# Lending input tiles to weight loads in the last mixer group of a two-layer backbone

## The chip, the cores and the metric

The kernel runs on one core of a Trainium2 chip. The metric is the device time of one execution in microseconds; three runs give a median. A profile of one further execution shows every instruction of the engines: TensorE (PE, its weight loads PEld), VectorE (DVE), ScalarE (ACT), GpSimd (POOL), and the queue of SyncE (SP or SPq), which issues nearly all transfers from HBM.

## The reference

Two layers of a trunk over 256 latent tokens and 256 context tokens of width 2048, with one batch. The first layer mixes by centred pooling, the second by neighbourhood attention; a gated MLP with a depthwise convolution of width 3 follows each (inner width 5504). Every sub-layer is preceded by an RMS norm and modulated by six vectors of 2048 per stream, which a product with `w_mod` gives. All is float32. What concerns the change is the first layer:

```python
def pool_mix(u, w, b, scale):          # windows 2, 4, 8, 16: four groups of 512 channels
    ...
    y = jnp.einsum('btgc,gcd->btgd', p, w).reshape(B, T, D) + b
    return y * scale

def conv_ffn(u, w_gate, w_up, conv_w, conv_b, w_down):
    gp = jnp.pad(u @ w_gate, ((0, 0), (1, 1), (0, 0)))
    gte = gp[:, :T] * conv_w[0] + gp[:, 1:T + 1] * conv_w[1] + gp[:, 2:] * conv_w[2] + conv_b
    return (jax.nn.silu(gte) * (u @ w_up)) @ w_down

ml = (silu_c @ w_mod[i] + b_mod[i]).reshape(B, 6, 1, D)
a_lat = modulate(rms_norm(h, norm1_g[i]), ml[:, 0], ml[:, 1])
h = h + ml[:, 2] * y_lat
h = h + ml[:, 5] * conv_ffn(modulate(rms_norm(h, norm2_g[i]), ml[:, 3], ml[:, 4]), ...)
```

The context stream `hc` goes through the same first layer with `silu_cc`.

## The kernel before, in words

Channels lie on the 128 partitions; the 16 tiles of 128 channels hold both streams side by side (512 columns). Each float32 operand of a large product is split in a high and a low part, and three matmuls (high by high, high by low, low by high) replace one. A weight load is a tile of 128 by 1024, 512 KB. `split` makes the high part by a cast on ScalarE (L143) and the low part by a subtraction on VectorE (L145).

The first layer is worked in four groups `g` of 512 channels, one for each pooling window. The modulation has 24 chunks of 512 outputs; a chunk is four quarters of two loads each (`wm`), multiplied on PE in strips of 32 columns (`mod`, L193), copied by ScalarE (`modev`, L198), and turned by four PE transposes (`modt`, L203). A row of the profile for `mod` counts two records for each matmul, so x8 is a whole quarter and x4 the half of one, that is, one load. `need(n)` has the modulation's generator run up to its n-th quarter. `mixer(g + 1)` prepares the next group's pooled input (tiles `ph`), multiplies by the pooling weights (`wp`, `pm`), adds to the streams, sums the squares for the second norm (`n2q`, `n2acc`), and leaves the group's four input tiles `Ad` in tiles A4g to A4g+3.

`partial(g, ...)` takes a group's input to the first eight tiles of the feed-forward's gate and up products, before the second norm is known. For the tiles 0 to 3 and then 4 to 7 it loads gate weights (`wcg`) and up weights (`wcu`), two loads of 512 KB each. Of the products, tiles 0 to 5 (`cg3_0` and so on) are added by VectorE into `part` (L558); tiles 6 and 7 (`cg_6`) stay in PSUM over all groups. Small products with the shift vectors (`pwg`, `pwu`, L528) use the unsplit loads and need `sh`, a copy of the shift chunk (12 to 15). A step is one tile of one of the two products; each is cut in two halves, and `between(half)` runs at the start of each half, 32 halves to a group: it asks for quarters of the modulation, takes a step of the mixer, and in the last group, from half 3, has the second norm finished (`n2s`, `n2b`, L299) and normalises the final inputs tile by tile (`normalise`, `nrm` L310, `A` L312 and L313) into the tiles A0 and up, one more every second half, so A4 from half 11 and A11 at half 25. GpSimd multiplies `part` by the norm (L352); gates follow at halves 16 to 25. The feed-forward's own loop (`gu0`, `g` and `u` L631 to L633) begins after the group; its two held tiles go through `late` (L355).

Loads take rooms in turn. There are six of their own (`wst`); `lend` adds tiles A that stand empty, and withdraws the others:

```python
    def lend(ks):
        rooms[:] = [r for r in rooms if r < 0 or r in ks] + [k for k in ks if k not in rooms]

    def stage(name):
        r = rooms.pop(0)
        rooms.append(r)
        if r >= 0:
            return ap0.tile([P, 1024], F32, tag=f"A{r}", name=name)
        return wst.tile([P, 1024], F32, tag=f"wst{-r}", name=name)
```

A load waits in the SP queue until the last reader of its room is done, and all loads behind it wait with it. Groups 0 to 2 have eight lent tiles beside the six (twelve ahead of group 0); at the last half of group 2 and in group 3 none is lent. The instructions are written in the order of these generators; the tile framework then sorts them by its own model of times, allots the rooms' waits, and each engine executes its list in that order.

Of the kernel before, what the change touches and what calls it, by code (L numbers as in the profile page):

```python
# [19 lines left out]
KT = D // P  # L20
# [16 lines left out]

NRH = 3
GATES = (16, 19, 22, 25)


_VEC = [
# [15 lines left out]
def kernel(ctx: ExitStack, tc: tile.TileContext, xT, cxT, wmod, wg, wu, wd, wp,  # L58
# [50 lines left out]
    def lend(ks):  # L109

        rooms[:] = [r for r in rooms if r < 0 or r in ks] + [k for k in ks if k not in rooms]
# [192 lines left out]
    def normalise(l, which, h_of, streams, rstd, pool, ks=range(KT), keep=A):  # L304

        for k in ks:
            a = ap0.tile([P, 2, 2, T], F32R, tag=f"A{k}", name=f"A{k}_{l}_{which}")
            y = pool.tile([P, 2, T], F32, tag="t2", name=f"nrm{l}{which}{k}")
            for s in streams:
                nc.vector.scalar_tensor_tensor(y[:, s], h_of(s)[:, k, :], M(l, which + 1, k, s),  # L310
                                               rstd[:, T * s : T * s + T], op0=ALU.mult, op1=ALU.mult)
                nc.scalar.activation(a[:, 0, s, :], y[:, s], AF.Identity, bias=M(l, which, k, s))  # L312
                ins = nc.vector.scalar_tensor_tensor(a[:, 1, s, :], y[:, s], M(l, which, k, s),  # L313
                                                     a[:, 0, s, :].bitcast(F32), op0=ALU.add, op1=ALU.subtract)
            keep[k] = a
            if l == 1 and k == 1:
                hold[:] = [ins.ins]
# [5 lines left out]
    with ExitStack() as ph0:  # L323
# [22 lines left out]
        def late(f):  # L346

            res = []
            for q in range(2):
                if f < NC:  # L350
                    r = PART[f][:, q]
                    nc.gpsimd.tensor_tensor(r, r, late_norm[0], op=ALU.mult)  # L352
                else:
                    r = f0.tile([P, 512], F32, tag="t2", name=f"late{f}_{q}")
                    nc.vector.tensor_tensor(r, HELD[f, q], late_norm[0], op=ALU.mult)  # L355
                for s in both:
                    v = r[:, T * s : T * s + T]
                    nc.scalar.activation(v, v, AF.Identity, bias=wsh[:, q, f, s : s + 1])
                res.append(r)
            return res  # L360

        def gate0(f, pg, pu):
            g1 = f0.tile([P, 2, T], F32, tag="t2", name=f"g1_{f}")
            nc.scalar.activation(flat(g1), pg, AF.Identity, scale=V("cw1_0")[:, f : f + 1], bias=V("cb_0")[:, f : f + 1])
            pg3 = pg.rearrange("p (s t) -> p s t", s=2)
            nc.vector.scalar_tensor_tensor(g1[:, :, 1:T], pg3[:, :, 0 : T - 1], V("cw0_0")[:, f : f + 1],
                                           g1[:, :, 1:T], op0=ALU.mult, op1=ALU.add)
            nc.vector.scalar_tensor_tensor(g1[:, :, 0 : T - 1], pg3[:, :, 1:T], V("cw2_0")[:, f : f + 1],
                                           g1[:, :, 0 : T - 1], op0=ALU.mult, op1=ALU.add)
            sg = f0.tile([P, 512], F32, tag="t2", name=f"sg_{f}")  # L370
            nc.scalar.activation(sg, flat(g1), AF.Silu)
            nc.vector.tensor_tensor(sg, sg, pu, op=ALU.mult)
            if f == NS - 1:
                a = mp.tile([P, 2, 512], F32R, tag="macc", bufs=1, name=f"act_{f}")
            else:
                a = act_tile(f"act_{f}", F32R)
            a = [a[:, 0], a[:, 1]]
            nc.scalar.copy(a[0], sg)
            nc.vector.tensor_tensor(a[1], sg, a[0].bitcast(F32), op=ALU.subtract)
            return a, sg  # L380
# [5 lines left out]
        with ExitStack() as phs:  # L386
# [45 lines left out]
            def need(n):  # L432
                while done[0] < n:
                    next(pump0, None)
                    done[0] += 1
# [4 lines left out]
            def mixer(g):  # L440
# [67 lines left out]
                yield  # L508

            def partial(g, sh, between):  # L510

                step = 0
                for fa in range(0, NS, 4):
                    for q, (nm, wsrc) in enumerate((("g", wg), ("u", wu))):
# [3 lines left out]
                        for j in range(4):  # L518
                            f = fa + j
                            between(2 * step)  # L520
                            if j == (3 if fa == 0 and q == 0 else 0):
                                need(20 * g + 21)
# [19 lines left out]
                            for i in range(4):  # L542
                                c = 512 * (j % 2) + P * i
                                xh, xl = flat(A[4 * g + i][:, 0]), flat(A[4 * g + i][:, 1])
                                nc.tensor.matmul(ps, hi[:, c : c + P], xh, start=(first and i == 0), stop=False)
                                nc.tensor.matmul(ps, hi[:, c : c + P], xl, start=False, stop=False)
                                nc.tensor.matmul(ps, lo[:, c : c + P], xh, start=False, stop=(final and i == 3))
                                if i == 1:
                                    between(2 * step + 1)
# [24 lines left out]
                next(mix)  # L574
            rstd = None
            for g in range(4):
                lend((range(8, KT), [*range(12, KT), *range(4)], range(8), ())[g])
                mix = mixer(g + 1) if g < 3 else None
                todo = [20 * g + 20 + n for n in STEPS] if g < 3 else []
                last = [14]  # L580
                F = {}
                rstd = n2.acc

                def between(half):
                    need(min(20 * g + LEAD + RATE * (half + 1) // 32, 20 * g + LEAD + PMAX))
                    if (g, half) == (2, 31):
                        lend(())
                    if g == 3 and half == NRH:
                        nc.scalar.copy(rstd, n2.rstd())
                        late_norm.append(rstd)  # L590
                    if todo and done[0] > todo[0] and half >= last[0] + 2:
                        last[0] = half
                        todo.pop(0)
                        next(mix)
                    k = (half - NRH) // 2
                    if g == 3 and 0 <= k < 12 and (half - NRH) % 2 == 0:
                        normalise(0, 3, h_of, both, rstd, f0, range(k, k + 1), keep=F)
                    if g == 3 and half in GATES:
                        e = GATES.index(half)
                        acts[e], _ = gate0(e, *late(e))  # L600

                partial(g, shs[g % 2], between)
                for n in todo:
                    need(n)
                    next(mix)
# [626 lines left out]
```

## Time and profile before

| what | value |
|---|---|
| time, median of three runs | 3102.35 us (3099.67 to 3103.05) |
| profiled execution, time | 3103.48 us |
| its span, first to last instruction | 3101.7 us |
| PE busy | 3030.0 us, 98% of the span |
| DVE, ACT, POOL busy | 1932.6, 1373.2, 826.1 us |
| moved from HBM | 554.93 MB, 180 GB/s over the span |

The span's start is zero for all times below. PE's busy share is near one nearly everywhere; where it idles, a view by stretches, the list of waits and the timelines of the engines tell. Group 3's first product begins near 352 us, and the feed-forward's loop at 454.54 us. Waits are put down to the instruction whose end came last. In a timeline, x counts merged records, and brackets give the idle time of the engine before a row and what ended it.

### The profile page before, as it was taken

Reading aid. Unit: us, or ns where it says so; the run is one execution under the profiler, and the core shown is the slowest. Engines: PE = TensorE matmul, PEld = TensorE weight load, DVE = VectorE, ACT = ScalarE, POOL = GpSimd, SP = SyncE. Lnnn points to the kernel's source line nnn. Section 1 sums busy time; section 2 is a strip of 40 time slices with the busy share of each in tenths; the row PEclk is TensorE's granted clock in tenths of the full one; section 3 lists DMA queues with packets and bytes.
Section 4 is the critical chain, followed back from the end, with each engine's and each line's share of the span. In section 5 each row is a group of like instructions: output and inputs, shape, how many; then the busy total and the mean of one; then the engine's idle time right before and its main releaser. Section 6 shows DMA issues by size and latency. Waiting matters only on the chain.

```text
span 3101.7 us, 40819 instructions
## 1 busy us (share of the span) xinstructions
PE 3030.0 (98%) x15082; PEld 2414.3 (78%) x15082; DVE 1932.6 (62%) x2748; ACT 1373.2 (44%) x2219; POOL 826.1 (27%) x823
## 2 busy tenths in 40 slices
PE   6999899999999999999999999999999999999998
PEld 2565558888888888888888788878788888888887
DVE  4445674285765848567485665564777666666666
ACT  3333454333233332323334444343545666656665
POOL 2011213213031230302213000000002466556665
PEclk9999999999999999999999999999999999999999
DMA  9978573264846657475573333332345565555563
GB/s 376 333 271 306 177 246 102 89 217 149 251 141 206 198 162 247 133 225 171 182 226 118 102 113 106 102 114 96 111 153 179 177 196 188 192 189 185 179 195 117
DMA packets 177927, 559.70 MB, mean 180 GB/s; under 512 B 17600, under 2 KB 22208, under 8 KB 177728
## 3 DMA queue, kind: packets, MB, share of 16 engines
q1 hardware_dynamic: 177728, 557.10, 55.0%
q8 instruction: 119, 1.95, 0.3%
q14 instruction: 80, 0.66, 0.1%
HBM read 554.93 MB, written 2.10 MB: 180 GB/s over the span
## 4 chain that ended last, share of the span: by engine, by line
PE 94%; DMA 2%; DVE 2%; POOL 1%; ACT 1%; issue 0%; SPq 0%; DVEq 0%; ACTq 0%; POOLq 0%
PE g L766 5%; PE u L766 5%; PE d L657 5%; PE d L659 5%; PE d L658 5%; PE d L813 4%; PE u L631 4%; PE u L632 4%; PE u L633 4%; PE g L631 4%; PE g L633 4%; PE g L632 4%; PE mod L193 3%; PE u L769 3%; PE g L769 3%; PE d L817 2%
## 5 line engine op out<-in xcount | busy, mean ns | idle before, releaser
L670 POOL TENSOR_TENSOR hl<-hl,dy 128x256 f32<-128x256 f32 x160 | 149.0, 931 | 958.6 <-ACT dy L669 957.3
L828 POOL TENSOR_TENSOR hl<-hl,dy 128x256 f32<-128x256 f32 x320 | 331.5, 1069 | 188.4 <-ACT dy L826 186.1
L241 DVE SCALAR_TENSOR_TENSOR macc<-wm,sc,macc 128x512 f32<-128x512 f32 (+1 forms) x360 | 325.2, 935 | 68.6 <-DMA wm<-wmod 67.6
L669 ACT ACTIVATE dy<-d,modT 128x256 f32<-128x256 f32 x320 | 133.5, 470 | 196.8 <-PE d L659 195.5
L193 PE MATMUL mod<-wm,sc 128*32 128x512 f32 x768 | 134.6, 618 | 26.6 <-DMA wm<-wmod 26.5
L670 POOL TENSOR_TENSOR hc<-hc,dy 128x256 f32<-128x256 f32 x160 | 126.0, 787 | 0.0
L145 DVE TENSOR_TENSOR wd_2l<-wd,wd_2h 128x1024 fp32r<-128x1024 f32 (+1 forms) x44 | 53.9, 1229 | 112.8 <-ACT wd_2h L143 112.8
L826 ACT ACTIVATE dy<-d,modT 128x512 f32<-128x512 f32 x160 | 104.4, 683 | 42.7 <-PE d L817 41.2
L915 POOL TENSOR_TENSOR rk<-rk,rp 128x256 f32<-128x256 f32 x16 | 13.2, 826 | 365.4 <-DVE rk L914 309.8
L145 DVE TENSOR_TENSOR wd_3l<-wd,wd_3h 128x1024 fp32r<-128x1024 f32 (+1 forms) x44 | 52.0, 1202 | 80.6 <-ACT wd_3h L143 80.6
L145 DVE TENSOR_TENSOR wd_1l<-wd,wd_1h 128x1024 fp32r<-128x1024 f32 (+1 forms) x44 | 53.7, 1224 | 58.6 <-ACT wd_1h L143 58.6
L466 POOL TENSOR_TENSOR pf<-ws,inv 128x256 f32<-128x256 f32 x32 | 27.7, 886 | 222.4 <-DVE ws L461 154.7
L193 PEld LDWEIGHTS mod<-wm,sc 128*32 128x32 f32 x768 | 23.6, 110 | 81.0 <-issue 59.4
L143 ACT CAST wd_1h<-wd 128x1024 fp32r<-128x1024 f32 (+1 forms) x44 | 45.2, 1029 | 79.8 <-PE u L632 50.6
L145 DVE TENSOR_TENSOR wd_0l<-wd,wd_0h 128x1024 fp32r<-128x1024 f32 (+1 forms) x44 | 54.6, 1247 | 40.7 <-ACT wd_0h L143 40.6
L1004 ACT ACTIVATE sb<-sb,nm 128x512 f32<-128x512 f32 x64 | 46.1, 721 | 64.4 <-DVE nm L1000 63.2
L143 ACT CAST wd_0h<-wd 128x1024 fp32r<-128x1024 f32 (+1 forms) x44 | 45.3, 1031 | 57.9 <-PE u L766 29.1
L792 DVE TENSOR_TENSOR actb<-sgb,actb 128x256 fp32r<-128x256 f32 x43 | 52.3, 1216 | 27.0 <-ACT actb L791 27.0
L657 PE MATMUL d<-act,wd_2h 128*128 128x512 f32 x172 | 68.0, 395 | 0.0
L658 PE MATMUL d<-act,wd_2h 128*128 128x512 f32 x172 | 67.9, 395 | 0.0
L657 PE MATMUL d<-act,wd_3h 128*128 128x512 f32 x172 | 67.9, 395 | 0.0
L657 PE MATMUL d<-act,wd_0h 128*128 128x512 f32 x172 | 67.9, 395 | 0.0
(1752 smaller groups left out, 9286.1 us busy)
## 6 DMA issues: line engine op xcount, KB each, us to landing
wm<-wmod SPq DMA_DIRECT2D x384, 512.0 KB, 6.1
wd<-wd SPq DMA_DIRECT2D x168, 512.0 KB, 4.4
wg<-wg SPq DMA_DIRECT2D x156, 512.0 KB, 4.6
wu<-wu SPq DMA_DIRECT2D x156, 512.0 KB, 4.5
wv<-wv SPq DMA_DIRECT2D x32, 512.0 KB, 3.9
wk<-wq SPq DMA_DIRECT2D x32, 512.0 KB, 4.0
wq<-wq SPq DMA_DIRECT2D x32, 512.0 KB, 3.7
wo<-wo SPq DMA_DIRECT2D x32, 512.0 KB, 4.4
```

Source lines behind the costliest of these rows:

```text
L145: eng.tensor_tensor(lo[:, :n], t[:, :n], hi[:, :n].bitcast(F32), op=ALU.subtract)
L193: nc.tensor.matmul(ps[32 * j : 32 * j + 32, :], sc[:, 4 * g + j, :], ts[j // 2][0][:, 512 * (j % 2) : 512 * (j % 2) + 512], start=(g == 0) ...
L241: nc.vector.scalar_tensor_tensor(acc[s], v, sc2[:, k, s : s + 1], acc[s], op0=ALU.mult, op1=ALU.add)
L631: nc.tensor.matmul(ps, hi[:, c : c + P], xh, start=(k == 0), stop=False)
L632: nc.tensor.matmul(ps, hi[:, c : c + P], xl, start=False, stop=False)
L633: nc.tensor.matmul(ps, lo[:, c : c + P], xh, start=False, stop=(k == KT - 1))
L657: nc.tensor.matmul(ps, hi[:, o : o + P], xh, start=(i == 0), stop=False)
L658: nc.tensor.matmul(ps, hi[:, o : o + P], xl, start=False, stop=False)
L670: nc.gpsimd.tensor_tensor(h_of(s)[:, k, :], h_of(s)[:, k, :], y[:, s], op=ALU.add)
L766: nc.tensor.matmul(ps, hi[:, c : c + P], flat(B[k]), start=(k == 0), stop=False)
L769: nc.tensor.matmul(ps[:, T:], lo[:, c : c + P], B[k][:, 0], start=False, stop=(k == KT - 1))
L828: nc.gpsimd.tensor_tensor(hl[:, k, :], hl[:, k, :], y[:, q], op=ALU.add)
```

## The change

At the last half of group 2 the eight tiles A4 to A11, the inputs of groups 1 and 2, are lent; from half 6 of group 3 only A8 to A11; from half 13 none. Before, nothing was lent from the last half of group 2 on. A4 is first written by the normalisation at half 11, A8 at half 19. No arithmetic is changed.

```diff
 NRH = 3
 GATES = (16, 19, 22, 25)
+
+LENT = {(2, 31): range(4, 12), (3, 6): range(8, 12), (3, 13): ()}
...
             for g in range(4):
-                lend((range(8, KT), [*range(12, KT), *range(4)], range(8), ())[g])
+                if g < 3:
+                    lend((range(8, KT), [*range(12, KT), *range(4)], range(8))[g])
                 mix = mixer(g + 1) if g < 3 else None
...
                 def between(half):
                     need(min(20 * g + LEAD + RATE * (half + 1) // 32, 20 * g + LEAD + PMAX))
-                    if (g, half) == (2, 31):
-                        lend(())
+                    if (g, half) in LENT:
+                        lend(LENT[g, half])
```

## The prediction

> **What bounds the kernel now.** The time before is 3102.35 us, the median of three runs from 3099.67 to 3103.05. The profiled execution took 3103.48 us, 1.13 more than the median, and 1.78 of it lie outside the span, which is the page's first line:
>
> ```profile
> span 3101.7 us, 40819 instructions
> ```
>
> I read the page first: TensorE (PE) is busy nearly everywhere, so a change to rooms for loads can only win where PE stands still. Next comes the view by stretches, over the stage that the change touches: from the first matmul of chunk 15 of the modulation to the first of the feed-forward's loop, 348 to 455 us. Columns: stretch, length, busy time of each engine, granted clock, share of the DMA engines, GB/s.
>
> ```profile
> core 0: us, PE busy (x) PEld busy (x) DVE busy (x) ACT busy (x) POOL busy (x), PEclk, DMA share, GB/s
> ...
> 362.00:376.00 14.00, 11.05 (x65) 6.62 (x67) 12.29 (x24) 4.25 (x9) 5.46 (x4) 1.00 0.31 111
> 376.00:392.00 16.00, 10.58 (x56) 5.90 (x50) 3.14 (x3) 5.69 (x11) 1.19 (x1) 0.79 0.77 261
> ...
> sum 107.00, PE 95.40 PEld 49.01 DVE 68.74 ACT 47.00 POOL 20.70; mean PE 15.90 PEld 8.17 DVE 11.46 ACT 7.83 POOL 3.45
> ```
>
> PE idles for 107.00 - 95.40 = 11.6 us, most of it from 362 to 392, where the DMA engines are first little used (0.31) and then crowded (0.77), and where the granted clock falls to 0.79. The list of waits of PE, from 360 to 456 us, accounts for all 11.6 (total, times, longest):
>
> ```profile
> PE pwu L528 <- DMA wcu<-wu: 5.4, 2, 4.1
> PE modt L203 <- ACT modev L198: 2.3, 2, 1.6
> PE pwg L528 <- ACT A L312: 1.6, 1, 1.6
> PE g L631 <- DVE late L355: 0.9, 1, 0.9
> PE mod L193 <- DMA wm<-wmod: 0.9, 2, 0.6
> PE n2b L299 <- DVE n2d L297: 0.5, 1, 0.5
> ```
>
> The queue's timeline (start, length of the issue, operation) tells why these weights are late:
>
> ```profile
> 349.90 0.33 SPq L127 DMA_DIRECT2D wm<-wmod  x1
> ...
> 369.83 0.33 SPq L127 DMA_DIRECT2D wm<-wmod  x1
> ...
> 376.20 0.38 SPq L127 DMA_DIRECT2D wcu<-wu  x1
> ```
>
> With six rooms, the load issued at 349.90 takes a room that PE has just left, the one at 369.83 the room of the group's gate weights, and `wcu` the room of that one: a chain of load, use, load in which PE is a link. `wcu` goes out at 376.20, and the pieces of PE that need it stand.
>
> **What the change does to it, by the built order of instructions.** Only the stretch from chunk 15 to the first two tiles of the feed-forward differs; every engine executes the same work. Eight loads take lent tiles: chunk 15's last two quarters in tiles 4 to 7, chunk 20's third in 8 and 9, the first `wcu` in 10 and 11. None lands in the four that stay lent longest: the rotation does not come round to them. So the effect is those eight loads, the six rooms left free by them, and a new order of what follows. PE's durations hold the rest of the prices:
>
> ```profile
> 340.40 0.39 PE L547 MATMUL cu<-Ad,wcu_4l 128*128 128x512 f32 x1
> ...
> 383.89 1.95 PE L528 MATMUL pwu<-wcu,sh 128*32 128x256 f32 x14 [4.13 <-DMA wcu<-wu]
> 385.77 0.80 PE L545 MATMUL cu<-Ad,wcu_0h 128*128 128x512 f32 x1
> ...
> 387.54 0.39 PE L547 MATMUL cu<-Ad,wcu_0l 128*128 128x512 f32 x1
> 387.76 0.40 PE L545 MATMUL cu<-Ad,wcu_0h 128*128 128x512 f32 x1
> ...
> 391.75 1.05 PE L193 MATMUL mod<-wm,sc 128*32 128x512 f32 x4
> 392.73 0.50 PE L546 MATMUL cu<-Ad,wcu_0h 128*128 128x512 f32 x1
> 393.07 0.40 PE L547 MATMUL cu<-Ad,wcu_0l 128*128 128x512 f32 x1
> ...
> 395.77 1.91 PE L193 MATMUL mod<-wm,sc 128*32 128x512 f32 x12
> ...
> 410.11 1.08 PE L528 MATMUL pwg<-wcg,sh 128*32 128x256 f32 x14
> ...
> 424.53 1.06 PE L193 MATMUL mod<-wm,sc 128*32 128x512 f32 x8
> ```
>
> The wait for `wcu`, 5.4 us. Tiles 10 and 11 come free with the last matmul of group 2 that reads them, the row at 340.40, which ends at 340.8. A load of `wcu` lands 5.5 us after its issue in the median here:
>
> ```profile
> wcu<-wu SPq DMA_DIRECT2D x4, 512.0 KB, 5.5
> ```
>
> So it is there at about 346.5. Before, PE came to it near 378 (383.89 less the two waits, 5.4, and the two matmuls between them), and it can come only a few microseconds sooner: over 25 us in hand. The wait goes: 5.4.
>
> The waits for `wm`, 0.9. Chunk 20's first and third quarters stand ahead of `wcu` in the queue, so they go out before 341; the second takes the rooms that are free at 349.90 and lands near 355.5. In the new order eight matmuls on each of two banks and the sums of the norm stand between chunk 15's end and the first of these, so PE needs none before about 359 (an estimate). Gone: 0.9.
>
> The clock. After the 4.1 us wait the 14 `pwu` took 1.95 us, where 14 of the same form take 1.08 (410.11): 0.87 lost. The four matmuls that follow took 387.54 - 385.77 = 1.77, where four take 4 x 0.22 (the step from 387.54 to 387.76) and 0.1 for the switch, 1.0: 0.77 lost. The longest wait left is 1.6 us, so I count 1.6 as won. The Trainium skill, "TensorE: Matmul & The Clock Gate", Part 1, says that the clock halves after about 3.4 us without work and returns after 3.4 us of it; its section on oscillation prices the throttled time at one half, which for two windows of 3.4 us would be an estimate of 3.4 us in place of my 1.6, and a gain 1.8 larger. I keep the rows, since part of the slow time fell on the wait itself.
>
> The wait for `n2d`, 0.5. Chunk 20's first three quarters now stand before the broadcast of the second norm on PE and cover DVE's chain. Gone; but the norm's result itself comes about 2 us later, since PE has 3 to 4 us of pieces in front. The wait before `pwg` (1.6) hangs on that norm's DVE work and on the copy of the shift: it stays, between 1 and 2; taken as unchanged.
>
> The waits for `modev`, 2.3. The first (0.7) was the copy of chunk 20 directly before its transposes; now eight matmuls, 1.8 us, stand between. The second (1.6) was ScalarE standing at the cast of the second `wcu` for its load, with the copy queued behind:
>
> ```profile
> 430.74 1.04 ACT L143 CAST wcu_4h<-wcu 128x1024 fp32r<-128x1024 f32 x1 [7.14 <-DMA wcu<-wu]
> ```
>
> In the new order the copy stands ahead of the cast, and six matmuls are between it and its transposes. Gone: 2.3.
>
> Pieces of the modulation. Half a quarter (x4, 1.05 us) costs as much as a whole (x8, 1.06), so cuts cost time. A piece set between other matmuls moves the second one after it to 393.07, where without it this would be 1.2 us earlier; a further quarter in the same piece adds 0.85 (1.91 for x12 less 1.06). Chunk 15's last quarter was two pieces and now joins the piece before: 2 x 1.2 - 0.85 = 1.55 won. Chunk 20's stays at two pieces, one of them newly between others: 0.2 lost. Chunks 20 (last) to 23 go from 21 pieces to 19 with the same units: 2 x 0.3 = 0.6 won. Sum 2.0 won; between 1 and 3.
>
> New waits. The load of chunk 15's last quarter now waits for DVE to be done with the pooling weights; chunk 15's second quarter is queued behind it on the queue. That split is done several microseconds before the queue moves on: nothing. The first half of `wcu`'s split now stands in the chain of the second norm (ScalarE 1.04 us for the cast): everything up to the tiles of group 3 comes 1.1 later there, covered by the 0.85 of the joined piece and a little slack: 0 to 0.3, taken as 0. The real one: the second `wcu`'s second half takes the room of a half of chunk 22 that now leaves PE in a later piece. From there to its use PE has about 5.6 us (two quarters 1.9, six matmuls 1.4, transposes 0.6 and 0.6, a quarter 1.1); landing takes 5.5 in the median: between 0 and 2, taken as 0.5, because the queue is quiet just then.
>
> What stays. The 0.9 before the feed-forward's first matmul: same order of DVE behind the last transposes.
>
> **The sum.** Waits 5.4 + 0.9 + 0.5 + 2.3 = 9.1; clock 1.6; pieces 2.0; less 0.5: 12.2 us. The profiled execution would be 3103.48 - 12.2 = 3091.3, the median 3102.35 - 12.2 = 3090.2. Bounds: with the low ends (clock 1.6, pieces 1, `wcu` 2, `pwg` 0.4 longer, 0.3 of the cast) 9.1 + 1.6 + 1 - 2.7 = 9.0; with the high ends 9.1 + 1.6 + 3 + 0.6 = 14.3.
>
> **The rivals.**
>
> The wait moves to the second `wcu`. The second half of the stage keeps six rooms and now runs on a PE that never pauses. Against: before, the same six rooms fed that half, and PE lost only the 1.6 us behind ScalarE's cast to them. For: the margin at the second `wcu` is near nothing, and PE comes to each room sooner. If PE waits there as long as it did for the second half of the first `wcu`, 4.1 us, and the clock's 1.6 is lost again, 12.7 - 5.7 = 7.0 us are won: 3095.3. Chance 0.17.
>
> VectorE becomes the bound. DVE is busy 68.74 us of 107.00; the stage would shrink to 95. Its normalisation stretches while GpSimd multiplies:
>
> ```profile
> 364.58 1.63 DVE L310 SCALAR_TENSOR_TENSOR nrm<-hl,modT,n2acc 128x256 f32<-128x256 f32 x1
> ...
> 367.64 0.47 DVE L310 SCALAR_TENSOR_TENSOR nrm<-hl,modT,n2acc 128x256 f32<-128x256 f32 x1
> ```
>
> 1.63 beside a product of GpSimd, 0.47 without. Twelve such products follow the norm; if each stretched two of DVE's instructions by 1.16 more than now, 28 us would be added, 2 more than DVE's 26 idle ones, and late starts in DVE's order would do the rest: some 8 us lost, 4 won, 3098.4, no difference that can be told. The Trainium skill, "GPSIMD Engine Reference", Specifications, says that GpSimd's SBUF interfaces are shared with VectorE and contended by instructions with two SBUF inputs; by it these two do collide, as the rows show. Against: most such meetings are in the 68.74 already. Chance 0.07.
>
> Slower: ScalarE stands in the second norm's chain. The cast of the first `wcu` is now before the last block of the sums of squares in ScalarE's order, at about 348.5. If its load were not there, ScalarE, then DVE, the norm and PE would wait one for one. It decides from a landing at 348.5, and it makes the kernel slower once the landing is past 348.5 + 12.2 = 360.7; at a landing of 370 it gives 3112. Against: issue near 339 to 341 by the row at 340.40, and few loads ahead. Chance 0.06.
>
> **How the numbers follow.** A measurement of this kernel can tell about 0.2%, 6.2 us. The forecast (9 to 14.3 won) has 0.70, the moved wait 0.17, both faster by more than that; VectorE 0.07, the same; ScalarE 0.06, slower. Faster 0.87, same 0.07, slower 0.06. Range: 14.3 won and 1.3 for the scatter of a median gives 3086.7; the other end reaches over the moved wait, to 3097.
>
> **What would show it.** Right: between 362 and 392 no wait of PE for `wcu` or `wm`; the clock 1.00 throughout; PE busy near 94 us of a stage near 95; `wcu` landed before 347; the first matmul of the feed-forward's loop about 12 us sooner in the span. A wait of PE for the second `wcu` above 1 us shows the first rival, waits of PE for DVE's `part` or `A` the second, ScalarE idle before its cast at 348 the third. The forecast is wrong if the stage shrinks by less than 9 us, or if it does and the later stages give it back.

## The result, and the profile after

The changed kernel took 3088.35 us, the median of six runs from 3086.2 to 3089.06, against 3101.76 us (3099.67 to 3104.05, six runs) for the kernel before, run on the same chip. The ratio is 0.9957, with a 95% interval of 0.9946 to 0.9968: 13.4 us won, where 12.2 were forecast. The profiled execution took 3089.06 us, 14.4 less than the one of before.

The page of the kernel after begins with the span, and its first part gives PE's busy time, which fell by 3.0 us while the span fell by 14.4: most of the gain is time in which PE had stood idle.

```profile
span 3087.3 us, 40828 instructions
...
PE 3027.0 (98%) x15082; PEld 2416.4 (78%) x15082; DVE 1932.3 (63%) x2748; ACT 1372.7 (44%) x2219; POOL 828.1 (27%) x823
```

The view by stretches, with the columns of the prediction's:

```profile
core 0: us, PE busy (x) PEld busy (x) DVE busy (x) ACT busy (x) POOL busy (x), PEclk, DMA share, GB/s
...
362.00:376.00 14.00, 12.43 (x88) 7.31 (x86) 11.70 (x21) 5.02 (x9) 4.18 (x3) 1.00 0.62 212
376.00:392.00 16.00, 16.00 (x87) 9.40 (x80) 10.63 (x20) 6.78 (x16) 5.49 (x4) 1.00 0.57 190
...
sum 93.00, PE 90.55 PEld 48.85 DVE 69.77 ACT 46.76 POOL 21.66; mean PE 15.09 PEld 8.14 DVE 11.63 ACT 7.79 POOL 3.61
```

From 376 to 392 PE is busy without a gap, where it had been busy for 10.58 of 16 us; the clock is 1.00 instead of 0.79; and the DMA engines, 0.31 and then 0.77 busy before, are evenly used (0.62, 0.57). The list of waits of PE is down to two lines, those that were forecast to stay:

```profile
engine line waited for: us in total, times, longest us
PE pwg L530 <- ACT A L314: 1.6, 1, 1.6
PE g L634 <- DVE late L357: 0.9, 1, 0.9
```

The timeline shows the shift products of the up weights without a wait in front, and the ends of the stage:

```profile
348.46 1.07 PE L195 MATMUL mod<-wm,sc 128*32 128x512 f32 x8
...
375.27 1.09 PE L530 MATMUL pwu<-wcu,sh 128*32 128x256 f32 x16
...
440.77 0.50 PE L634 MATMUL g<-A,wg_8h 128*128 128x512 f32 x1 [0.88 <-DVE late L357]
```

From here on "the stage" is the time from chunk 15's first matmul to the first of the feed-forward's loop. It was 454.54 - 347.95 = 106.6 us before and is 92.3 after: 14.3 less. What lies behind it took 2647.2 us before and 2646.5 after, so nothing was given back. (Over all fourteen traces that part runs from 2645.1 to 2649.9 us, so a loss of a microsecond or two could hide in it.)

The start of the stage scatters: up to there PE has the same list in both kernels, and yet the stage began at 347.95, 348.46 and, in another execution of the changed kernel, at 346.90. The stage itself was 92.31 and 92.38 in those two executions. The experiments are therefore read by their stage first and by their time second. They ran on three chips; each ratio is to the kernel before on the same chip, whose median was 3101.9, 3102.5 and 3102.1 us there.

### The profile page after: what moved, and what is told of

Its sections match the earlier page's. It is cut to its first block, busy times and chain, and to the rows that moved or that the text cites. A ratio compares the mean times of both kernels' runs of the same rounds, so it can differ in the third digit from the quotient of the medians.

```text
span 3087.3 us, 40828 instructions
## 1 busy us (share of the span) xinstructions
PE 3027.0 (98%) x15082; PEld 2416.4 (78%) x15082; DVE 1932.3 (63%) x2748; ACT 1372.7 (44%) x2219; POOL 828.1 (27%) x823
## 4 chain that ended last, share of the span: by engine, by line
PE 94%; DVE 2%; POOL 1%; DMA 1%; ACT 1%; issue 1%; SPq 0%; DVEq 0%; ACTq 0%; POOLq 0%
PE g L769 5%; PE u L769 5%; PE d L660 5%; PE d L662 5%; PE d L661 5%; PE d L816 4%; PE u L634 4%; PE u L635 4%; PE u L636 4%; PE g L634 4%; PE g L636 4%; PE g L635 4%; PE mod L195 3%; PE u L772 3%; PE g L772 3%; PE d L820 2%
```

## The experiments

The theory was that PE stood for loads that had no room, so that every room counts. Its rivals were that the one late `wcu` is the whole cause, or that the new order of the instructions brings the gain, whoever gets the rooms.

| kernel | stage us | waits of PE in it | rest | starts, stretches | time us (median) |
|---|---|---|---|---|---|
| before | 106.6 | 11.6 | 95.0 | 31, 72 | 3101.8 |
| the change | 92.3 | 2.5 | 89.8 | 31, 65 | 3088.4 |
| eight until half 6 | 94.3 | 3.7 | 90.6 | 30, 72 | 3088.9 |
| four until 13 | 88.2 | 2.5 | 85.7 | 27, 63 | 3085.2 |
| `wcu` alone | 100.9 | 7.2 | 93.7 | 33, 74 | 3095.4 |
| `wm` alone | 92.2 | 3.7 | 88.5 | 29, 64 | 3086.7 |
| before, quarters whole | 106.6 | 16.2 | 90.4 | 28, 60 | 3104.7 |
| change, quarters whole | 89.6 | 4.5 | 85.1 | 26, 57 | 3086.9 |
| four, quarters whole | 90.1 | 4.7 | 85.4 | 25, 58 | 3085.9 |
| the same, `sh` later | 89.5 | 6.0 | 83.5 | 24, 55 | 3086.3 |
| four until 18 | 86.7 | 2.9 | 83.8 | 26, 57 | 3081.5 |
| eight until 10, four until 18 | 88.6 | 3.0 | 85.6 | 27, 60 | 3085.1 |
| two until 13 | 100.5 | 8.3 | 92.2 | 30, 66 | 3097.8 |

Waits are the sum of PE's list over the stage; the rest is the stage less the waits. "Starts" counts, in the built order, how often PE begins a quarter of the modulation or takes one up again after other work; "stretches" counts runs of matmuls of one kind.

**The later four tiles.** The prediction said that no load lands in the four tiles that stay lent from half 6. Without them:

```diff
-LENT = {(2, 31): range(4, 12), (3, 6): range(8, 12), (3, 13): ()}
+LENT = {(2, 31): range(4, 12), (3, 6): ()}
```

> The eight tiles A4 to A11 are lent at the last half of group 2 and withdrawn at half 6; the later four are dropped. The stage is counted from chunk 15's first matmul to the feed-forward's first: 106.6 us before, 92.3 after. The prediction said that no load lands in the four lent longest; if so, nothing changes: stage 92.3, time 3088. Theory now (each room counts, and PE stands where a load is late): the built order shows chunk 20's third quarter and the first wcu back in own rooms; wcu then goes out when chunk 20's first quarter is done, near 363, lands near 369, before PE needs it near 375; chunk 20's third quarter takes the gate weights' room, goes out near 372, lands near 377 to 378, and PE waits 1 to 3 for it. Stage 94 to 95.5, time 3090 to 3092. Rival (it is the early wcu in tiles 10 and 11 that wins): wcu waits as before, stage 101 or more, time 3097 or more.

The stage was 94.3 us, 2.0 longer than with them; the time was 3088.9 (ratio to before 0.9954, 0.9937 to 0.9970), which cannot be told from the change. The waits of PE:

```profile
PE g L634 <- DVE late L357: 1.9, 1, 1.9
PE pwg L530 <- ACT A L314: 1.6, 1, 1.6
PE mod L195 <- DMA wm<-wmod: 0.2, 1, 0.2
```

In the built order chunk 20's third quarter and the first `wcu` lose their lent tiles, so they did land in A8 to A11 under the entry of half 6: that sentence of the prediction was wrong. Yet `wcu` in own rooms is in time, and the 2.0 us are 1.2 more waiting and 0.8 in the rest. The rival of the early `wcu` (stage of 101 or more) falls. The stage does not show all that this kernel loses: behind the wait of 1.9 us at its end the granted clock was 0.50 from 440 to 443, in stretches of 1 us.

**Four tiles in place of eight.**

```diff
-LENT = {(2, 31): range(4, 12), (3, 6): range(8, 12), (3, 13): ()}
+LENT = {(2, 31): range(8, 12), (3, 13): ()}
```

> Four tiles, A8 to A11, lent from the last half of group 2 to half 13, in place of eight. By the built order chunk 20's first two quarters land in them, chunk 15's last quarter is again late and cut in two, wcu takes the rooms of chunk 15's third quarter and goes out near 353. Theory (each room counts): wcu lands near 359, no wait for it; lost against the change as built are the two pieces (1.5), the wait for n2d (0.5) and 1 to 2 for chunk 20's third quarter behind the gate weights: stage 95 to 96.5, time 3091 to 3093. Rival (any new order does it, the number of rooms does not matter): stage 92 to 93, time 3088.

Both expectations failed: the stage was 88.2 us, 4.2 shorter than with eight (time 3085.18, ratio 0.9942, 0.9927 to 0.9956). Its waits are those of the change, 1.6 us before `pwg` and 0.9 before the loop.

So the 4.2 us are work, not waiting. The built order has 27 starts instead of 31. A half quarter uses two of the four strips of columns and takes as long as a whole one, 0.98 us from 391.75 to 392.73 in the prediction's rows. A change of kind costs 0.11: the step behind it, from 392.73 to 393.07, is 0.34 us, where it is 0.23 inside a run. That leaves 0.87 for a start. Four starts and two stretches less give 3.5 + 0.2 = 3.7 of the 4.2. The traces bear the first term out: counted from the start of each matmul to the start of the next, less the waits, the modulation holds PE for 29.5 us in the change and for 26.0 here. The prediction had such a price for a cut; what it lacked was that the order that is built, and not the number of rooms, sets how many cuts there are.

**Which loads need the tiles.** Two kernels split the change: the first `wcu` alone in A10 and A11, and the modulation's loads alone.

```diff
-LENT = {(2, 31): range(4, 12), (3, 6): range(8, 12), (3, 13): ()}
+LENT = {(2, 31): ()}
+SPARE = {"wcu3_0_0": 10, "wcu3_0_1024": 11}
...
     def stage(name):
+        if name in SPARE:
+            return ap0.tile([P, 1024], F32, tag=f"A{SPARE[name]}", name=name)
         r = rooms.pop(0)
```

> Nothing is lent in group 3, but the first wcu's two loads get tiles A10 and A11; all modulation loads keep the six rooms. Theory (sum of the waits): the 5.4 and the clock's 1.6 are won, chunk 15's last quarter stays in two pieces, the wait for n2d (0.5) stays, chunk 20's first quarter waits 0 to 1.5 behind the gate weights: stage 97 to 99, time 3092 to 3095, some 7 to 9 us of the 13.4. Rival 1 (the late wcu is the whole cause): stage 92 to 94, time 3088 to 3090. Rival 2 (PE waits for the modulation's loads in place of wcu): stage 101 or more.

```diff
-        r = rooms.pop(0)
+        own = name.startswith("wcu3_0_")
+        r = rooms.pop(next(i for i, r in enumerate(rooms) if r < 0) if own else 0)
```

> The change as built, except that the first wcu takes own rooms, those of the gate weights, and chunk 20's last quarter gets tiles 10 and 11 instead. Theory: wcu goes out when the shift products of the gate weights are done, near 372.4, and its halves land near 377.3 and 378.7; PE comes to them near 375.3 and waits 2 to 3.5 in all, too short for the clock to fall; the pieces' gain stays: stage 94 to 96, time 3090.5 to 3092.5. Rival 1 (the late wcu is the whole cause): wait 5.4 and the clock's 1.6 as before, stage 99 or more, time 3095 or more. Rival 2 (rooms for the modulation alone do it): stage 92 to 93.

PE's waits with `wcu` alone:

```profile
PE n2b L304 <- DVE n2d L302: 1.7, 1, 1.7
PE pwg L533 <- ACT A L317: 1.6, 1, 1.6
PE modt L208 <- ACT modev L203: 1.5, 2, 0.7
PE g L637 <- DVE late L360: 0.9, 1, 0.9
PE cg L550 <- ACT Ad L507: 0.7, 1, 0.7
PE pwu L533 <- DMA wcu<-wu: 0.6, 1, 0.6
PE mod L198 <- DMA wm<-wmod: 0.2, 1, 0.2
```

and with the modulation alone:

```profile
PE pwg L531 <- ACT A L315: 1.6, 1, 1.6
PE g L635 <- DVE late L358: 0.9, 1, 0.9
PE pwu L531 <- DMA wcu<-wu: 0.8, 1, 0.8
PE cu L548 <- ACT wcu_0h L146: 0.4, 1, 0.4
```

`wcu` alone won 5.7 us of the stage (100.9; time 3095.36, ratio 0.9979, 0.9969 to 0.9989), less than the 7.6 to 9.6 expected: the wait for `n2d` grew from 0.5 to 1.7, 1.5 of the 2.3 for `modev` stayed, and there are two more starts. The modulation alone won all of it (92.2; time 3086.73, ratio 0.9947, 0.9932 to 0.9961), more than expected: its waits are 1.2 us above those of the change, and its rest, with two starts fewer, 1.3 below. The queue's timeline says why `wcu` did not need a tile of its own:

```profile
369.35 0.89 SPq L130 DMA_DIRECT2D wcu<-wu  x2
```

Both halves are out by 370.24, right behind the gate weights' shift products and 6.0 us before the second half went out in the kernel before (376.20), because chunk 20's first quarter no longer stands between the two in the chain of load, use, load. For `wcu` one link taken out was enough, and it need not be its own. For the stage as a whole it does matter which loads get the rooms: two tiles for `wcu` left 7.2 us of waits, the tiles for the modulation 3.7.

**Fewer cuts.** If cuts are what is left, the order inside a quarter should help: a quarter that begins with the later of its two loads can hardly start before both are there. The edit was put on the kernel before, on the change, and on the kernel with four tiles; a fourth kernel moved the first shift products behind tile 3 as well (all of the diff but its first change).

```diff
-            for j in range(4):
+            for j in (2, 3, 0, 1):
                 nc.tensor.matmul(ps[32 * j : 32 * j + 32, :], sc[:, 4 * g + j, :],
...
-                            if j == (3 if fa == 0 and q == 0 else 0):
+                            def shifts():
...
+                                return ev
+
+                            late_pw = g == 3 and fa == 0 and q == 0
+                            if j == (3 if fa == 0 and q == 0 else 0) and not late_pw:
+                                ev = shifts()
...
                                 if i == 1:
                                     between(2 * step + 1)
+                                    if late_pw and j == 3:
+                                        ev = shifts()
```

> The kernel before, nothing lent in group 3; only the order of the four matmuls of a quarter of the modulation is changed, so that the two that use the later load come first. A quarter can then hardly start before both loads are there, and is cut less often: by the built order 28 starts of a quarter or a part of one in the stage instead of 31, and 60 stretches of like matmuls instead of 72. Theory now (time of the stage is waits, plus 0.87 us for each started quarter or part, plus about 0.11 for each change between kinds): 3 x 0.87 + 12 x 0.11 = 3.9 less at equal waits, stage 102 to 104 against 106.6; the wait for wcu stays. Rival (rooms and waits alone set the stage, cuts are free): 106 to 107.

> The change as built with the same order inside the quarters: 26 starts instead of 31, 57 stretches instead of 65. Theory: 5 x 0.87 + 8 x 0.11 = 5.2 less, stage 86 to 88.5 against 92.3; time 3082 to 3085. Rival (cuts are free): 92 to 93; or it trades the cuts for waits on the later loads, stage 90 or more with new waits of PE for wm.

> Four tiles lent (A8 to A11, from the last half of group 2 to half 13; stage 88.2 in its earlier run) with the same order inside the quarters: 25 starts instead of 27, 58 stretches instead of 63. Theory: 2 x 0.87 + 5 x 0.11 = 2.3 less, stage 85 to 87, time 3081 to 3084. Rival: 88 to 89.

> As the one before, and the first shift products of the gate weights in group 3 are written half a tile later; in the built order they stand behind the twelve matmuls of tile 3 instead of before them. Theory: the wait of 1.6 us behind the copy of the shift goes (2.8 us of matmuls now cover it), 24 starts and 55 stretches: 1.6 + 0.9 + 0.3 less than the one before, stage 82 to 84, time 3078 to 3082. Rival: the transposes behind them wait for ScalarE's copy of the products instead (up to 1.5), stage 84 to 86.

The kernel before did not gain: 106.6 us, as the rival had it, time 3104.65 (ratio 1.0007, 0.9998 to 1.0017). The first lines of its waits:

```profile
PE pwu L528 <- DMA wcu<-wu: 6.7, 2, 5.0
PE mod L193 <- DMA wm<-wmod: 2.5, 2, 2.1
PE modt L203 <- ACT modev L198: 1.8, 3, 0.7
PE n2b L299 <- DVE n2d L297: 1.8, 1, 1.8
```

Its rest fell by 4.6 us as the theory has it (3.9), and its waits rose by the same 4.6: where the loads are late, time saved on cuts was waited out. On the change the stage fell by 2.7 instead of 5.2 (89.6; 3086.88, ratio 0.9953, 0.9939 to 0.9968): 4.7 of work less, 2.0 of waits more. On four tiles it grew by 1.9 (90.1; 3085.86, ratio 0.9951, 0.9936 to 0.9966), with 2.2 more waiting. In the fourth kernel (89.5; 3086.26, ratio 0.9952, 0.9935 to 0.9969) the wait of 1.6 us before `pwg` is gone, and others take its place, of which its rival had named only the last, the 0.8 before `ptg`:

```profile
PE pwu L530 <- DVE part L567: 1.7, 1, 1.7
PE n2b L301 <- DVE n2d L299: 1.2, 1, 1.2
PE modt L205 <- ACT modev L200: 1.2, 2, 0.8
PE g L641 <- DVE late L357: 0.9, 1, 0.9
PE ptg L570 <- ACT peg L534: 0.8, 1, 0.8
```

The price of a start held in the first two (4.6 for 3.9, 4.7 for 5.2; in the second, counted from start to start as above, the modulation held PE for 24.9 us instead of 29.5, where five starts price at 4.4), and roughly in the fourth, with its 2.2 of work less than four tiles alone instead of 3.5. In the third the rest fell by 0.3 only, where 2.3 were expected: there the clock fell, as the last section shows. The assumption "at equal waits" held in none, and all four stages came out longer than forecast.

**Longer, fewer, and once more.** The last four kernels change only the tiles and the halves; the fourth is the change as it stands.

```diff
-LENT = {(2, 31): range(4, 12), (3, 6): range(8, 12), (3, 13): ()}
+LENT = {(2, 31): range(8, 12), (3, 18): ()}                            # four until 18
+LENT = {(2, 31): range(4, 12), (3, 10): range(8, 12), (3, 18): ()}     # eight until 10, four until 18
+LENT = {(2, 31): range(10, 12), (3, 13): ()}                           # two until 13
```

> Four tiles, A8 to A11, lent from the last half of group 2 and kept until half 18, one before the first of them is written again; the order inside a quarter is as in the change. Built order: 26 starts of quarters or parts, 57 stretches (four tiles until half 13: 27 and 63, stage 88.2). Theory (starts at 0.87, changes at 0.11, waits as before): 0.9 + 0.7 = 1.5 less, stage 86 to 88, time 3082 to 3086. Rival (rooms past half 13 only move waits to the queue's later loads): 88 to 90.

> Eight tiles until half 10, then A8 to A11 until half 18. Built order: 27 starts, 60 stretches, against 31 and 65 of the change. Theory: 4 x 0.87 + 5 x 0.11 = 4.0 less than the change's 92.3 at equal waits, stage 87.5 to 89.5, time 3083 to 3087: eight tiles are no better than four. Rival (more rooms, less time): below 86.

> Only A10 and A11 lent, from the last half of group 2 to half 13: eight rooms instead of six, for whichever load comes round to them. Built order: 30 starts, 66 stretches. Theory: 6 us less work than before (0.87 + 6 x 0.11 and the clock's 1.6, less shift products cut), and the late loads' waits halved: stage 93 to 98, time 3090 to 3095. Rival (two tiles suffice): 92 or less.

> The change as built, once more, on the same chip as the three others, for a direct comparison and for the scatter of the stage between executions: stage 92 to 92.6, time 3086 to 3089. If the stage differed by more than 0.5 between executions of one program, differences of a few us between the stages above would not count.

Four tiles until half 18 gave a stage of 86.7 us and a time of 3081.51 (3080.49 to 3082.8; ratio 0.9934, 0.9921 to 0.9946). On the same chip the change took 3087.15 (3086.53 to 3088.53; ratio 0.9953, 0.9940 to 0.9965), so this version beats both kernels, the change by 5.6 us. Its waits:

```profile
PE pwg L530 <- ACT A L314: 1.6, 1, 1.6
PE g L634 <- DVE late L357: 1.0, 1, 1.0
PE n2b L301 <- DVE n2d L299: 0.3, 1, 0.3
```

They are those of the change but for 0.4; the stage is 5.6 shorter, with 5 starts and 8 stretches less (5 x 0.87 + 8 x 0.11 = 5.2). Eight tiles until half 10 came to 88.6 (3085.10, ratio 0.9943, 0.9929 to 0.9956), also as priced. These two stages were forecast from the counts of the built order, and fell inside.

Two tiles came to 100.5 us (3097.80, ratio 0.9986, 0.9978 to 0.9995), longer than expected, and not for late loads of `wcu` or `wm`, for which PE never waits there:

```profile
PE pwg L530 <- issue: 5.7, 1, 5.7
PE g L634 <- ACT wu_8h L145: 2.0, 1, 2.0
PE pwg L530 <- DMA wcg<-wg: 0.6, 1, 0.6
```

The profile names no releaser for the 5.7 us. `pwg` needs `sh`, and VectorE's timeline in this kernel has its copy at 369.21:

```profile
364.22 1.40 DVE L312 SCALAR_TENSOR_TENSOR nrm<-hl,modT,n2acc 128x256 f32<-128x256 f32 x1
365.54 1.48 DVE L312 SCALAR_TENSOR_TENSOR nrm<-hc,modT,n2acc 128x256 f32<-128x256 f32 x1
...
368.21 0.67 DVE L560 TENSOR_TENSOR part<-part,cg 128x512 f32<-128x512 f32 x1
368.81 0.47 DVE L315 SCALAR_TENSOR_TENSOR A<-nrm,modT,A 128x256 fp32r<-128x256 f32 x1
369.21 1.23 DVE L419 COPY sh<-modT 128x8 f32<-128x8 f32 x1
```

The copy ends at 370.44 and `pwg` begins at 370.54; that the one waited for the other is read from these times, not from a releaser. In the new order more normalisation and a sum stand ahead of the copy, and the one tile of matmuls in front of `pwg` was over by 364.83. The granted clock was 0.76 from 362 to 376 in this kernel.

Taken together, none of the three readings holds alone. The late `wcu` is not the whole cause, since early loads of it won 5.7 us of 14.3. A new order without rooms won nothing (before, quarters whole). And rooms do not simply count, since four tiles beat eight: once the long waits are gone, the order that is built decides the rest.

## Why the prediction was right, point by point

**Waits, 9.1 forecast, 9.1 measured.** PE's list fell from 11.6 to 2.5 us: `wcu` 5.4, `wm` 0.9, `n2d` 0.5 and `modev` 2.3 are gone, the 1.6 before `pwg` and the 0.9 before the loop stay. `wcu` went out from 339.74 on and landed within 4.9 us in the median, before the 347 that was named. But the reason given for the largest term was too narrow. The tiles 10 and 11 mattered little to it: with `wcu` in own rooms and tiles for the modulation alone PE waits 0.8 us for it and 0.4 for its cast, and the stage is the same, 92.2.

**Clock, 1.6 forecast, 1.6 to 1.7 by the trace.** The granted clock is 1.00 through the stretches that showed 0.79, and the rows that carried the 1.64 are back at 1.09 for `pwu`. A finer view of the kernel before shows where the slow time lay (columns as above):

```profile
380.00:384.00 4.00, 0.11 (x4) 0.11 (x8) 1.22 (x1) 0.23 (x2) 0.00 (x0) 0.57 0.87 268
384.00:388.00 4.00, 4.00 (x21) 2.33 (x21) 1.23 (x1) 1.50 (x2) 0.00 (x0) 0.58 0.83 302
```

In the second stretch PE worked all the time, and 0.42 x 4 = 1.7 us went. In the first the clock was as low, but PE stood, and 0.43 x 4 = 1.7 more cost next to nothing. The two together are the estimate of 3.4 that the prediction worked out from the Trainium skill, "TensorE: Matmul & The Clock Gate", section on oscillation, and set aside: the slow clock withheld as much as that, but half of it fell on the wait, which was the prediction's reason. The prediction's other figure from there, 3.4 us without work before the clock falls, does not fit this trace: the clock was at 0.50 from 381 on, in stretches of 1 us, when the long wait had lasted since 379.76 and the 1.29 us before it had been parted from it by 0.59 us of work.

The rest of the stage less 0.87 for each start and 0.11 for each stretch is 55 to 57 us in the nine kernels that kept their clock in it (mean 56.0), and 60.1, 59.4 and 58.8 in the three that lost it in a long wait (before, before with whole quarters, two tiles); the kernel with four tiles and whole quarters, whose clock fell without a long wait, is at 57.3. The slow clock is a part of that surplus; cuts made by the waits themselves are another, as the next point shows.

**Pieces, 2.0 forecast, 3.5 left: the term that was mis-sized.** The stage lost 14.3; less 9.1 and 1.6, some 3.5 are left, with nothing spent on the second `wcu`. The step counted pieces of the modulation in the built order. The modulation's starts are in fact 31 in both orders; what fell is the number of stretches of all kinds, 72 to 65 (0.8 at 0.11 each), and cuts that stand in no built order, because a wait made them:

```profile
373.82 1.05 PE L193 MATMUL mod<-wm,sc 128*32 128x512 f32 x4 [0.63 <-DMA wm<-wmod]
375.11 2.77 PE L193 MATMUL mod<-wm,sc 128*32 128x512 f32 x20 [0.23 <-DMA wm<-wmod]
379.17 0.59 PE L528 MATMUL pwu<-wcu,sh 128*32 128x256 f32 x2 [1.29 <-DMA wcu<-wu]
...
408.47 0.62 PE L193 MATMUL mod<-wm,sc 128*32 128x512 f32 x2
408.48 0.62 PE L528 MATMUL pwg<-wcg,sh 128*32 128x256 f32 x2
```

The first two rows are three quarters of the modulation of which the first broke in its middle, as its second load came 0.23 us late: they held PE for 1.06 and 2.77 us, 3.8 together, where three unbroken ones come to 3 x 0.87 + 0.11 = 2.7. That is 1.1 lost beside the waits. The first two records of `pwu` stood apart and held PE for 0.59, while the other fourteen take 1.08 at full clock (410.11), as long as sixteen in one. The first two of a `pwg` stood apart as well, but they cost nothing: they ran side by side with half a quarter, and from 408.47 to the next matmul at 409.45 it is 0.98, what half a quarter takes alone. So 0.8 + 1.1 + 0.6 = 2.5 of the 3.5 are found; the last 1.0 was not resolved.

**Second `wcu`, 0.5 forecast, 0 measured.** Its second half landed at 419.38 in the trace of after, and PE came to it at 419.53 without a wait: a margin of 0.15 us, as narrow as was said. That it fell on the good side was luck as much as foresight.

**Where the tiles go.** "None lands in the four that stay lent longest" was wrong, as the kernel without the later entry shows: four loads do. The sentence also contradicts the one before it, which puts chunk 20's third quarter and `wcu` in 8 to 11. It cost the sum nothing, since the sum took these loads in the right tiles.

**The signs.** "PE busy near 94 us of a stage near 95" became 89.8 of 92.3; by the prediction's own terms, with 2.5 us of old waits and 0.5 of a new one left, it should have read 92. The other signs came as named, and the feed-forward began 13.8 us sooner.

**The rivals.** The wait did not move to the second `wcu`. ScalarE did not stand before the cast, as `wcu` landed before 348.5. VectorE did not become the bound in the change, but the rival was a real one: with two tiles it was, by the times of the copy, VectorE's queue and not a load that held PE for 5.7 us and took the clock with it, and only 6.1 us of the stage were won.

## What to carry to other kernels

When loads take rooms in turn, look for the chain of load, use, load in which the bound engine is a link, and take out a link. The late load itself need not get the spare room, but the choice is not free: rooms for the modulation's loads won 14.4 us of this stage, two tiles for the late `wcu` 5.7. More rooms can cost time through the order that a scheduler then builds; four tiles beat eight by 4.2 us. After the waits are gone, count the starts and changes of kind in the built order: at 0.87 us for a start and 0.11 for a change they forecast two stages here to within 0.5 us. Where the new order brought new waits or a lower clock, the forecasts made with the same count fell short: five stages came out 1.1 to 5.5 us beyond the top of their range. Compare stages, not whole times, when the effect is a few tenths of a per cent, and look past the stage's end, where a wait can still lower the clock.

## What the runs showed that was not expected

A copy of 128 by 8 elements on VectorE took 1.23 us (369.21 in the kernel with two tiles), while GpSimd had a product under way from 368.96 for 1.45 us. In the changed kernel the same copy took 0.16:

```profile
370.61 0.16 DVE L419 COPY sh<-modT 128x8 f32<-128x8 f32 x1
```

In all thirteen other traces it took 0.15 or 0.16, with no product of GpSimd beside it. So a size of almost nothing is no protection: the copy on which PE waits took nearly eight times as long in the one trace where GpSimd was at work, and it ended at 370.44, when the product ended at 370.41. No run put the two together on purpose.

The granted clock fell without a long wait as well. In the kernel with four tiles and whole quarters the longest wait of PE near 354 was 0.66 us, yet the view by stretches shows:

```profile
349.00:352.00 3.00, 3.00 (x19) 1.42 (x15) 2.96 (x9) 2.35 (x6) 1.01 (x2) 1.00 0.66 173
352.00:355.00 3.00, 2.34 (x14) 1.08 (x13) 2.12 (x6) 1.68 (x5) 0.00 (x0) 0.86 0.72 206
355.00:358.00 3.00, 3.00 (x10) 2.35 (x9) 0.00 (x0) 0.00 (x0) 0.00 (x0) 0.57 0.95 323
```

At 0.86 and 0.57 of full speed, 0.14 x 3 + 0.43 x 3 = 1.7 us of clock went there, which is most of the 2.0 us of work that this kernel failed to win. What PE did at that time were sums of single columns and half quarters, and the waits among them were short.

The prediction counted the clock as safe as long as no wait is longer than 1.6 us. This kernel contradicts that, and so does another; no length of a single wait parts the cases. The kernel before with whole quarters has the clock at 0.51 and 0.50 from 454 to 457, right behind its stage, after waits of 0.73 and 0.88 us with eight transposes between them. With whole quarters on the change, and in the fourth kernel of that series, a wait of 1.7 us left it at 1.00; one of 1.9, with eight tiles until half 6, did not. What lowers the clock, beyond the long waits, was not tried.
